# Projections of w_in as three products of scaled float16 parts instead of fp32r parts, with power-of-two scales found for four weight tiles at a time

## The chip, the cores and the metric

The kernel runs on one core of one Trainium2 chip. The metric is the device time of one execution, in microseconds (us). Engines are named as in the profile: PE is TensorE, with PEld for its weight loads, DVE is VectorE, ACT is ScalarE, POOL is GpSimd, and SP is SyncE, which here only issues transfers. Each engine runs its own instructions in the order in which they stand; ACT and POOL also issue transfers from their own queues.

## The reference

One encoder block over 1040 tokens (16 meta tokens and 1024 of x), width 1024. What the change touches is the first product, `proj`, of the normalized tokens with `w_in`, 1024 by 9280, and the five things cut from it:

```python
u = rms_norm(h, w_norm_mix[l])
proj = jnp.einsum('btd,dk->btk', u, w_in[l])
conf_a, conf_g = proj[..., 0:1024], proj[..., 1024:2048]
z, xbc = proj[..., 2048:4096], proj[..., 4096:7168]
dt_raw, gates = proj[..., 7168:7232], sigmoid(proj[..., 7232:])
c = silu(layer_norm(depthwise_conv(conf_a * sigmoid(conf_g), w_conf_dw[l], b), ...))   # 31 taps
branch_conf = einsum('btc,cd->btd', c, w_conf_out[l])
xbc = silu(depthwise_conv(xbc, w_ssm_conv[l], b))                                       # 7 taps
y = bidir_ssd(xs, dt_raw, ...)          # chunked scan over 9 chunks, both directions, 4 groups of 8 heads
branch_ssm = einsum('btc,cd->btd', rms_norm(y * silu(z), w_ssm_norm[l]), w_ssm_out[l])
h = h + einsum('btd,de->bte', gates[:1024] * branch_conf + gates[1024:] * branch_ssm, w_out[l])
h = h + expert_choice_ffn(rms_norm(h, ...), ...)        # 16 experts, 130 tokens each
return rms_norm(h[:, 16:], w_norm_final)
```

All inputs and the output are float32.

## The kernel before

The program is written in the order of the stages below, and a scheduler (it has its own model of the machine) fixes the order of the instructions on each engine before the run; `high_priority(offset=n)` lets it place work as if it had been written n steps earlier. On the chip each engine then runs its list in that order and waits by semaphores.

**Start.** Nine token tiles (`TOK`: 16, then 8 times 128) are loaded as `xt`, the odd ones from ACT's queue, the even ones from SP's. ACT squares each (`scr`, `ss`), DVE scales it, PE transposes it (`tp`), and it is split into two parts: `uh`, ACT's copy of the transpose in fp32r, and `ul`, DVE's difference (lines 186 and 187).

**Projection stage.** A weight tile is 1024 rows by 128 columns of `w_in`, held as 128 x 8 x 128. `load_w` (line 143, SP's queue, pool `wraw` of three) loads it, and `split_w` turns it into `wh` (ACT, line 151) and `wl` (DVE, line 152) in pool `wsp`, which has two of each. `proj` then makes, for each of three chunks of tokens (348, 346, 346), the 24 matmuls of `mm3`: for each of 8 slices, wh x uh, wh x ul, wl x uh (lines 96 to 98), all into one of the three PSUM buffers `mm`. 45 tiles come first: the dt tile, then four rounds of two conformer tiles (`do_conf`), six xbc tiles (`do_xbc`), two gate tiles and one z tile. The results leave PSUM by ACT (`pre`, `sg`, `st`) or DVE (`ci`). DVE does the convolutions: 30 taps over 1040 columns for each conformer tile (line 235, `co<-ci`), spread between other work by `some_taps`, and six for each xbc tile (line 340, `po<-pre`).

**Scan stage.** Four groups, each nine steps of two directions (`half`, at high priority). A half loads `row` (SP's queue, a broadcast of `cs_d`) and `xk`, `Bk` (ACT's queue); ACT makes `E` from `row` (lines 428 and 429), DVE multiplies `E` and `row` (lines 447 and 432), PE makes `cb`, `py` and `st_ps`, DVE and POOL carry the state `S`. After each step one item of `filler` is written: the other 28 weight tiles (4 conformer pairs, 12 z, 8 gates), in the program's order conformer, z, gates of that group. At the end of a group DVE multiplies by the z rows (`row<-row,xs`) and stores `yz_d`.

**After the scan.** `y_group` reloads `yz_d` rows as `yst` (two buffers, ACT's queue), splits each to `yh` (ACT) and `yl` (DVE), squares it (ACT) and adds it to `ssq` (POOL). `w_ssm_out` (32 tiles of 512 rows) and `w_conf_out` go through `load_w` and `split_w` as above and through `mm3` in fp32r. Beside it DVE does the conformer's layer norm (`mean`, `var`, `cc`). Then come `w_out`, the router, and 16 experts, whose products already use scaled float16 parts.

Names for the places spoken of later: the *last conformer tile* is the one of group 3, the *last gates* are two gate tiles written behind it, and the *hand-over* is the stretch from the last projection of `w_in` to the first product of `w_ssm_out`.

## Time and profile before

| | us |
|---|---|
| three timed runs | 3055.07, 3058.41, 3068.24; median 3058.41 |
| profiled execution, its own time | 3062.95 |
| its span, first to last instruction | 3061.2 |
| PE busy in the span | 2830.0 (92%) |
| DVE busy | 2216.2 (72%) |
| ACT busy | 1578.6 (52%) |

The span falls into stages: the start to about 42 us, projections to about 580, a pass of 25 us into the scan, the scan from about 605 to 1226, the hand-over and `w_ssm_out`, `w_conf_out`, `w_out` and the router to about 1700, then the experts to 3000. A busy share over the whole span mixes these, so the rows below are taken stage by stage. Matmuls are pipelined: a matmul's own duration covers more than its share of PE, and what counts is the distance between the starts of matmuls that follow each other.

### The profile page before, as it was taken

The page shows a single profiled execution, that of the slowest core. Times are in us where ns is not written, and L with a number is a line of the kernel's source. Part 1 is how long each engine was busy: PE and PEld are TensorE (multiplying, and loading weights), DVE is VectorE, ACT ScalarE, POOL GpSimd, SP SyncE. Part 2 cuts the span into 40 slices and gives each one's busy share as a digit, 9 for nine tenths or more (in the row PEclk, how much of TensorE's full clock was granted, in tenths as well). Part 3 has the DMA queues.
Part 4 walks back from the last instruction along what each step waited for, and adds up shares of the span by engine and source line. Part 5 has one row for each costly group of instructions (what it writes and reads, how often), then busy time and mean ns, then how long its engine had stood idle before and what let it go on. Part 6 is the DMA issues. An engine that isn't in the chain of part 4 may idle for free. (4 is left out here: it accounts for less than half of the span.)

```text
span 3061.2 us, 65630 instructions
## 1 busy us (share of the span) xinstructions
PE 2830.0 (92%) x28079; PEld 2693.4 (88%) x28079; DVE 2216.2 (72%) x2703; ACT 1578.6 (52%) x2351; POOL 722.2 (24%) x661
## 2 busy tenths in 40 slices
PE   7999999898888888899999789999999999999996
PEld 7999999786777676898978789999999999999995
DVE  7958669498696886989545678666767677767673
ACT  4433333454645564444213466666666666666643
POOL 1101011154354545322000002121222222222213
PEclk9999999899999899999999899999999999999998
DMA  4324233666868786442433879999999999999994
GB/s 123 108 90 133 72 124 99 165 144 167 183 170 205 178 192 133 156 141 80 154 119 115 298 285 327 320 320 328 329 325 339 330 324 333 332 321 333 343 325 139
DMA packets 425971, 665.99 MB, mean 218 GB/s; under 512 B 29217, under 2 KB 213953, under 8 KB 425673
## 3 DMA queue, kind: packets, MB, share of 16 engines
q1 hardware_dynamic: 366032, 514.83, 53.2%
q0 software_dynamic: 25760, 73.27, 7.9%
q10 hardware_dynamic: 33888, 73.71, 7.5%
q8 instruction: 220, 3.60, 0.5%
q14 instruction: 71, 0.58, 0.1%
HBM read 585.15 MB, written 76.59 MB: 216 GB/s over the span
## 5 line engine op out<-in xcount | busy, mean ns | idle before, releaser
L96 PE MATMUL gu<-xT,wh 128*128 128x130 f16 x3968 | 703.9, 223 | 4.3 <-ACT sil L952 3.8
L97 PE MATMUL gu<-xT,wh 128*128 128x130 f16 x3968 | 703.5, 221 | 0.0
L98 PE MATMUL gu<-xT,wl 128*128 128x130 f16 x3968 | 702.8, 221 | 0.6 <-DVE wl L923 0.4
L909 ACT ACTIVATE junk<-wst 128x2048 bf16<-128x2048 f32 x248 | 473.7, 1910 | 388.8 <-DMA wst<-in_w_exp_gate_dram 311.9
L96 PE MATMUL mm<-uh,wh 128*128 128x346 f32 (+2 forms) x1752 | 582.9, 333 | 14.5 <-ACT wh L151 12.2
L923 DVE SCALAR_TENSOR_TENSOR wl<-wst,sc,wh 128x2048 f16<-128x2048 f32 x248 | 572.8, 2346 | 24.2 <-ACT wh L920 21.0
L97 PE MATMUL mm<-ul,wh 128*128 128x346 f32 (+2 forms) x1752 | 579.7, 331 | 0.3 <-DVE ul L187 0.3
L98 PE MATMUL mm<-uh,wl 128*128 128x346 f32 (+2 forms) x1752 | 578.5, 331 | 0.2 <-DVE wl L152 0.2
L975 PE MATMUL dn<-ac,wst 128*128 128x130 f32 x3840 | 459.8, 277 | 0.0
L975 PEld LDWEIGHTS dn<-ac,wst 128*128 128x128 f32 x3840 | 441.1, 191 | 0.0
L97 PEld LDWEIGHTS <-wh 128*128 128x128 f16 x3968 | 394.4, 99 | 8.3 <-issue 6.8
L994 POOL DMA_INDIRECT h<-yo,idx x60 | 181.7, 3029 | 921.3 <-DVE yo L993 770.6
L96 PEld LDWEIGHTS <-wh 128*128 128x128 f16 x3968 | 388.9, 98 | 2.6 <-ACT wh L920 2.4
L98 PEld LDWEIGHTS <-wl 128*128 128x128 f16 x3968 | 386.6, 97 | 0.9 <-DVE wl L923 0.9
L96 PEld LDWEIGHTS mm<-uh,wh 128*128 128x128 f32 x1752 | 336.2, 192 | 29.4 <-ACT wh L151 14.0
L97 PEld LDWEIGHTS mm<-ul,wh 128*128 128x128 f32 x1752 | 336.6, 192 | 12.8 <-issue 11.8
L98 PEld LDWEIGHTS mm<-uh,wl 128*128 128x128 f32 x1752 | 335.5, 192 | 11.6 <-issue 10.4
L235 DVE SCALAR_TENSOR_TENSOR co<-ci,cp,co 128x1040 f32<-128x1040 f32 x240 | 343.1, 1429 | 1.7
L428 ACT ACTIVATE E<-row,cst 128x128 f32<-128x128 f32 (+1 forms) x576 | 170.2, 378 | 190.2 <-DMA row<-cs_d 171.7
L920 ACT ACTIVATE wh<-wst,sc 128x2048 f16<-128x2048 f32 x124 | 241.2, 1995 | 23.5 <-DVE sc L886 22.8
L151 ACT ACTIVATE wh<-wr 128x1024 fp32r<-128x1024 f32 (+1 forms) x113 | 105.6, 934 | 243.6 <-PE mm L97 196.1
L420 POOL TENSOR_TENSOR xw<-xk,dtw 128x512 f32<-128x512 f32 (+1 forms) x136 | 190.9, 1408 | 168.5 <-DMA xk<-xk_d 81.8
(329 smaller groups left out, 4572.1 us busy)
## 6 DMA issues: line engine op xcount, KB each, us to landing
wst<-in_w_exp_gate_dram SPq DMA_DIRECT2D x128, 1024.0 KB, 7.9
wst<-in_w_exp_up_dram SPq DMA_DIRECT2D x128, 1024.0 KB, 10.3
wst<-in_w_exp_down_dram SPq DMA_DIRECT2D x128, 1024.0 KB, 8.8
wr<-in_w_in_dram SPq DMA_DIRECT2D x73, 512.0 KB, 4.7
row<-cs_d SPq DMA_DIRECT2D x64, 512.0 KB, 9.0
xk<-xk_d ACTq DMA_DIRECT2D x64, 256.0 KB, 5.7
xbc_d<-po POOLq DMA_DIRECT2D x24, 520.0 KB, 3.0
xk_d<-xt POOLq DMA_DIRECT2D x20, 512.0 KB, 3.9
```

Source lines behind the costliest of these rows:

```text
L96: pe.matmul(ps, wh(k), xh(k), start=(k == 0), stop=False)
L97: pe.matmul(ps, wh(k), xl(k), start=False, stop=False)
L98: pe.matmul(ps, wl(k), xh(k), start=False, stop=(k == K - 1))
L151: act.activation(out=wh[:, :K], in_=r, func=AF.Copy)
L235: dve.scalar_tensor_tensor(co, ci[:, m:m + T], cp[:, j, m:m + 1], co, op0=OP.mult, op1=OP.add)
L420: pool.tensor_mul(heads(o[:L]), heads(xk[:L]), dtw[:L, c, w, hs].unsqueeze(2).to_broadcast([L, HG, 64]))
L428: act.activation(out=E[:L, j, :L], in_=row[:L, j, :L], func=AF.Relu, scale=-1.0, bias=cs)
L909: act.activation(out=junk, in_=t[m][b], func=AF.Square, accum_out=sq[:, b, m:m + 1])
L920: act.activation(out=wh[m][0], in_=t[m][0], func=AF.Copy, scale=sc[:, 1, m:m + 1])
L923: dve.scalar_tensor_tensor(wl[m][b], t[m][b], sc[:, 1, m:m + 1], wh[m][b], op0=OP.mult, op1=OP.subtract)
L975: pe.matmul(last["dn"][b // 3][:, b % 3], t[:, k, b * P:b * P + P], ac[:, 2 * i + k], start=(i + k == 0 and b % 3 == 0), stop=(i == 7 and ...
L994: nc.gpsimd.indirect_dma_start(out=h2_d[b], in_=yo[:, h], in_offset=None, compute_op=OP.add, out_offset=bass.IndirectOffsetOnAxis(ap=r.idx ...
```

## The change

The token parts and the weight parts of the 73 tiles of `w_in` become float16. To keep them in float16's range, each is multiplied by a power of two first: the tokens by one from the largest `w_norm_mix` (`power`, tile `su`), each weight tile by one from the sum of its squares. The class `Columns` holds the order of all 73 tiles. `group` loads four tiles (SP's queue, pool `r16` of eight), squares each on ACT with an accumulated sum, sums over partitions with one small PE matmul, and derives the scales with six small DVE instructions. `convert` makes `wh` and `wl`. `take` converts one tile ahead and asks for a group one group ahead. The inverse scale goes into instructions that already scale or copy (tanh, the copies of dt and xbc, the taps through `ct`, the z rows through `zinv`). `w_ssm_out` and `w_conf_out` keep fp32r and `split_w`; their pool `wsp` is now opened after the scan stage instead of at the start.

```diff
     wraw = wstack.enter_context(tpool("wraw", bufs=3))
-    wsp = wstack.enter_context(tpool("wsp", bufs=2))
...
+    def power(dst, src, up, down):
+        dve.tensor_scalar(dst[:, down], src, 32.0, 2.0 ** -110, op0=OP.mult, op1=OP.max)
...
-        uh = upool.tile([P, KD, T], FR, name="uh")
-        ul = upool.tile([P, KD, T], FR, name="ul")
+        uh = upool.tile([P, KD, T], F16, name="uh")
+        ul = upool.tile([P, KD, T], F16, name="ul")
...
+            def group(self):
+                b = 4 * self.groups
+                cols = self.order[b:b + 4]
...
+                for i, col in enumerate(cols):
+                    t = r16.tile([P, KD, P], F32, name="wr16")
+                    nc.sync.dma_start(t, w_in[0][:, col:col + P].rearrange("(k p) c -> p k c", p=P))
+                    act.activation(out=junk, in_=t, func=AF.Square, accum_out=sq[:, i:i + 1])
+                    self.raw[b + i] = t
+                sqb = w16.tile([P, 4], BF, name="sqb")
+                dve.tensor_copy(sqb[:, :n], sq[:, :n])
+                ps = mps.tile([P, 512], F32, name="mm")
+                pe.matmul(ps[:, :n], onesb, sqb[:, :n], start=True, stop=True)
...
+            def convert(self, n):
...
+                with tc.high_priority(offset=400):
+                    act.activation(out=wh, in_=t, func=AF.Copy, scale=sc[:, 1:2])
+                    dve.scalar_tensor_tensor(wl, t, sc[:, 1:2], wh, op0=OP.mult, op1=OP.subtract)
+                self.split[n] = wh, wl, sc
+
+            def take(self, col):
...
+                if n == 0:
+                    self.group()
+                    self.convert(0)
+                if n % 4 == 0:
+                    self.group()
+                self.convert(n + 1)
...
+        r16 = ostack.enter_context(tpool("r16", bufs=8))
+        w16 = ostack.enter_context(tpool("w16", bufs=2))
...
+            act.activation(out=wabs, in_=wmix, func=AF.Abs)
...
-                    act.activation(out=uu, in_=ps[:, :, :L], func=AF.Copy)
-                    dve.tensor_sub(ul[:, 4 * q:4 * q + 4, t0:t0 + L], ps[:, :, :L], uu.bitcast(F32))
+                    act.activation(out=uu, in_=ps[:, :, :L], func=AF.Copy, scale=su[:, 0:1])
+                    dve.scalar_tensor_tensor(ul[:, 4 * q:4 * q + 4, t0:t0 + L], ps[:, :, :L], su[:, 0:1], uu,
+                                             op0=OP.mult, op1=OP.subtract)
...
+    wsp = wstack.enter_context(tpool("wsp", bufs=2))
     right = ctx.enter_context(ExitStack())
```

**Start, ACT.** ACT's list while the first full token tiles are transposed and copied, before:

```order
L186 ACTIVATE uh<-tp 128x4x128
L151 ACTIVATE wh<-wr 128x1024
L186 ACTIVATE uh<-tp 128x4x128
L174 DMA xt<-in_x_dram 128x1024
L186 ACTIVATE uh<-tp 128x4x128 x2
L177 ACTIVATE scr,ss<-xt 128x1024
L186 ACTIVATE uh<-tp 128x4x128
```

And now, with numbers on the weight tiles (`wr_495` to `wr_504` are the first group, `wr_523` to `wr_532` the second):

```order
L192 ACTIVATE junk,sq<-wr_501 128x1024
L277 ACTIVATE uh<-tp,su 128x4x128 x2
L192 ACTIVATE junk,sq<-wr_504 128x1024
L277 ACTIVATE uh<-tp,su 128x4x128
L192 ACTIVATE junk,sq<-wr_523 128x1024
L277 ACTIVATE uh<-tp,su 128x4x128
L265 DMA xt<-in_x_dram 128x1024
L192 ACTIVATE junk,sq<-wr_526 128x1024
L217 ACTIVATE wh<-wr_495,sc 128x1024
L217 ACTIVATE wh<-wr_498,sc 128x1024
L217 ACTIVATE wh<-wr_501,sc 128x1024
L192 ACTIVATE junk,sq<-wr_529 128x1024
```

Squares of weight tiles now stand between the token copies; one more square of the second group, two of the third and four of token tiles follow before the next token copy.

**Start, PE.** Before, the first product of `w_in` stood behind the transposes of the first tokens:

```order
L184 MATMUL tp<-ident,xt 128x16 x8
L184 MATMUL tp<-ident,xt 128x128 x20
L96 MATMUL mm<-uh,wh 128x272
L184 MATMUL tp<-ident,xt 128x128 x4
L97 MATMUL mm<-ul,wh 128x272
```

Now both first groups' sums of squares stand ahead of it:

```order
L275 MATMUL tp<-ident,xt 128x16 x8
L275 MATMUL tp<-ident,xt 128x128 x24
L197 LDWEIGHTS onesb
L197 MATMUL mm<-sqb,onesb 128x4
L197 LDWEIGHTS onesb
L197 MATMUL mm<-sqb,onesb 128x4
L96 LDWEIGHTS wh
L96 MATMUL mm<-uh,wh 128x272
```

The first product moved behind the squares of eight weight tiles.

**Hand-over, DVE.** The list of DVE from the last conformer tile's `ci` on; `co<-ci` are its 30 taps, `wl<-wr,wh 128x512` is a tile of `w_ssm_out`. Before:

```order
L230 SCALAR_TENSOR_TENSOR ci<-sg,mm 128x346
L152 TENSOR_TENSOR wl<-wr,wh 128x1024
L235 SCALAR_TENSOR_TENSOR co<-ci,cp,co 128x1040 x4
L565 SCALAR_TENSOR_TENSOR yl<-yst,cp,yh 128x1040
L235 SCALAR_TENSOR_TENSOR co<-ci,cp,co 128x1040
L565 SCALAR_TENSOR_TENSOR yl<-yst,cp,yh 128x1040
L235 SCALAR_TENSOR_TENSOR co<-ci,cp,co 128x1040
L152 TENSOR_TENSOR wl<-wr,wh 128x512
L235 SCALAR_TENSOR_TENSOR co<-ci,cp,co 128x1040 x3
```

Now, from the first `yl` on (directly ahead of it stand the same `ci` and 17 taps):

```order
L663 SCALAR_TENSOR_TENSOR yl<-yst,cp,yh 128x1040
L329 SCALAR_TENSOR_TENSOR co<-ci,ct,co 128x1040
L663 SCALAR_TENSOR_TENSOR yl<-yst,cp,yh 128x1040
L329 SCALAR_TENSOR_TENSOR co<-ci,ct,co 128x1040 x5
L663 SCALAR_TENSOR_TENSOR yl<-yst,cp,yh 128x1040
L329 SCALAR_TENSOR_TENSOR co<-ci,ct,co 128x1040
L663 SCALAR_TENSOR_TENSOR yl<-yst,cp,yh 128x1040
L329 SCALAR_TENSOR_TENSOR co<-ci,ct,co 128x1040 x5
L663 SCALAR_TENSOR_TENSOR yl<-yst,cp,yh 128x1040
L329 SCALAR_TENSOR_TENSOR co<-ci,ct,co 128x1040
L663 SCALAR_TENSOR_TENSOR yl<-yst,cp,yh 128x1040 x2
L159 TENSOR_TENSOR wl<-wr,wh 128x512 x2
```

The first `wl` of `w_ssm_out` stood behind 6 taps and 2 `yl`; it now stands behind all 30 taps (17 and the 13 shown) and 7 `yl`. The pool `wsp` now lies where the scan stage's tiles lay: in the built program its first `wl` occupies bytes 46368 to 50464 of a partition, and `ci` bytes 47392 to 51672.

## Rows read from the trace of the kernel before

**Rows 1.** Windows by stage: length, busy us (instructions) by engine, PEclk, DMA, GB/s.
```profile
0.00:42.00 42.00, 26.60 (x182) 23.83 (x182) 30.51 (x52) 28.20 (x54) 10.62 (x110) 1.00 0.66 185
42.00:580.00 538.00, 536.06 (x3420) 531.72 (x3421) 407.87 (x354) 186.91 (x297) 54.83 (x133) 1.00 0.34 104
605.00:1226.00 621.00, 529.60 (x4124) 453.40 (x4125) 499.91 (x619) 339.92 (x786) 305.10 (x261) 0.93 0.74 173
1226.00:1250.00 24.00, 24.00 (x153) 24.00 (x153) 22.48 (x16) 10.43 (x13) 8.34 (x5) 1.00 0.64 204
1250.00:1300.00 50.00, 40.40 (x229) 39.25 (x228) 49.30 (x34) 23.19 (x37) 19.81 (x7) 0.90 0.41 128
```
**Rows 2.** Windows, wh x uh matmuls alone (line 96): PE, PEld, clock, DMA.
```profile
42.00:580.00 538.00, 346.75 (x1072) 201.61 (x1072) 1.00 0.34 104
605.00:1226.00 621.00, 204.13 (x582) 116.07 (x583) 0.93 0.74 173
```
**Rows 3.** Waits of PE from 42 to 580: waiter, releaser, total, times, longest.
```profile
PE mm L96 <- ACT wh L151: 1.9, 5, 0.4
```
**Rows 4.** Timeline of PE, projections, 348 and 346 columns: start, duration, what.
```profile
299.77 0.32 PE L97 MATMUL mm<-ul,wh 128*128 128x348 f32 x1
...
305.97 0.32 PE L97 MATMUL mm<-ul,wh 128*128 128x346 f32 x1
```
**Rows 5.** Timeline of PE, the dt tile's first chunk, 272 columns.
```profile
20.19 0.29 PE L98 MATMUL mm<-uh,wl 128*128 128x272 f32 x1
...
22.83 0.29 PE L98 MATMUL mm<-uh,wl 128*128 128x272 f32 x1
```
**Rows 6.** Timeline of PE, an expert's float16 products, 130 columns.
```profile
2630.16 0.22 PE L96 MATMUL gu<-xT,wh 128*128 128x130 f16 x1
...
2630.96 0.22 PE L98 MATMUL gu<-xT,wl 128*128 128x130 f16 x1
```
**Rows 7.** Costliest groups by form, ACT: count, busy, mean ns, idle before.
```profile
L151 ACT ACTIVATE wh<-wr 128x1024 fp32r<-128x1024 f32 x81 | 85.5, 1056 | 198.3 <-PE mm L97 168.5 <-DMA row<-sz_d 12.6 <-POOL xw L420 8.8
L177 ACT ACTIVATE scr<-xt 128x1024 f32<-128x1024 f32 x8 | 8.5, 1058 | 1.9 <-DMA xt<-in_x_dram 1.6 <-DVE xt L179 0.2
L177 ACT ACTIVATION_READ_ACCUMULATOR scr<-xt 128x1 f32 x8 | 1.6, 194 | 0.0
```
**Rows 8.** The same for DVE.
```profile
L923 DVE SCALAR_TENSOR_TENSOR wl<-wst,sc,wh 128x2048 f16<-128x2048 f32 x248 | 572.8, 2346 | 24.2 <-ACT wh L920 21.0
L152 DVE TENSOR_TENSOR wl<-wr,wh 128x1024 fp32r<-128x1024 f32 x81 | 108.6, 1341 | 67.5 <-ACT wh L151 67.1 <-PE mm L98 0.2
L888 DVE TENSOR_SCALAR sc<-sc,sx 128x2 f32<-128x2 f32 x62 | 13.9, 224 | 0.0
```
**Rows 9.** Timeline of PE, the first conformer product.
```profile
42.39 0.43 PE L96 MATMUL mm<-uh,wh 128*128 128x348 f32 x1 [0.18 <-ACT wh L151]
```
**Rows 10.** Waits of SP's queue from 605 to 1226, the largest.
```profile
SPq L143 <- DVE wl L152: 126.5, 19, 19.4
```
**Rows 11.** Waits of ACT from 605 to 1226, the largest.
```profile
ACT E L428 <- DMA row<-cs_d: 157.9, 49, 10.5
```
**Rows 12.** Waits of PE from 605 to 1226, the largest.
```profile
PE py L454 <- DVE E L447: 18.3, 13, 5.9
```
**Rows 13.** Timeline of DVE at the hand-over.
```profile
1227.35 0.52 DVE L230 SCALAR_TENSOR_TENSOR ci<-sg,mm 128x346 f32<-128x346 f32 x1 [0.15 <-PE mm L98]
...
1235.52 1.30 DVE L565 SCALAR_TENSOR_TENSOR yl<-yst,cp,yh 128x1040 fp32r<-128x1040 f32 x1 [0.84 <-ACT st L249]
```
**Rows 14.** Windows, the taps alone (line 235): DVE, clock, DMA.
```profile
1226.00:1250.00 24.00, 13.87 (x9) 1.00 0.64 204
1250.00:1300.00 50.00, 37.16 (x21) 0.90 0.41 128
```
**Rows 15.** Timeline of ACT, first `yh` of the first two pairs.
```profile
1233.48 1.17 ACT L564 ACTIVATE yh<-yst,cp 128x1040 fp32r<-128x1040 f32 x1 [1.60 <-DMA yst<-yz_d]
1246.01 1.17 ACT L564 ACTIVATE yh<-yst,cp 128x1040 fp32r<-128x1040 f32 x1 [3.02 <-DMA yst<-yz_d]
```

More of the change, by code (lines that the diff above doesn't have):

```diff
@@ new lines, in tile_block @@
+        order = [OFF_DT]
+        for i in range(4):
+            order += [i * P, D + i * P]
+            for m, j in enumerate((4 * i, 4 * i + 1, 4 * i + 2, 4 * i + 3, 16 + i, 20 + i)):
+                order.append(OFF_XBC + j * P)
+                if m in (2, 5):
+                    order.append(OFF_GATE + (2 * i + (m == 5)) * P)
+            order.append(OFF_Z + i * P)
+        for g in range(GR):
+            order += [(4 + g) * P, D + (4 + g) * P]
+            order += [OFF_Z + j * P for j in range(4 + 4 * g, min(8 + 4 * g, 16))]
+            order += [OFF_GATE + j * P for j in range(8 + 2 * g, 10 + 2 * g)]
@@ L168, in tile_block @@
+        columns = Columns(order)
+        wtile = columns.take
+        r16 = ostack.enter_context(tpool("r16", bufs=8))
+        w16 = ostack.enter_context(tpool("w16", bufs=2))
         with tpool("a_sb", bufs=2) as sb, tpool("a_ps", bufs=4, space=PSUM) as aps:
@@ L227, in do_conf @@
                 sg = cfp.tile([P, 348], F32, name="sg", bufs=2)
-                act.activation(out=sg[:, :n], in_=pg, func=AF.Tanh, scale=0.5)
+                act.activation(out=sg[:, :n], in_=pg, func=AF.Tanh, scale=wg[3])
                 pa = proj(wa, t0, n)
@@ L248, in gate_tile @@
                 ps = proj(w, t0, n)
-                act.activation(out=st[:, t0:t0 + n], in_=ps, func=AF.Tanh, scale=0.5)
+                act.activation(out=st[:, t0:t0 + n], in_=ps, func=AF.Tanh, scale=w[3])
             nc.gpsimd.dma_start(gate_d[j], st)
@@ L335, in do_xbc @@
                     ps = proj(w, t0, n)
-                    act.activation(out=pre[:, 3 + t0:3 + t0 + n], in_=ps, func=AF.Copy)
+                    act.activation(out=pre[:, 3 + t0:3 + t0 + n], in_=ps, func=AF.Copy, scale=w[2])
                 po = b1.tile([P, T], F32, name="po")
```

69 lines of the change are left out of this document (54 added, 15 removed).

## The prediction

> **What bounds the kernel now.** I read the windows by stage first, then the waits of the engine that is full, then the distances between its matmuls. The projection stage from 42 to 580 us is PE's alone: PE is busy 536.06 of 538 us at full clock [rows 1] and waits 1.9 us in all [rows 3]. DVE, at 407.87 us, is 76% busy beside it. In the scan, 605 to 1226, no engine is full: PE 529.60 of 621 us (85%), DVE 499.91 (80%), ACT 339.92 (55%) [rows 1]. There the halves follow each other through ACT, DVE and PE in turn, and the projections fill gaps. ACT's largest wait is for the `row` transfers, 157.9 us [rows 11], and SP's queue, which issues them, stands 126.5 us before weight loads whose buffer is not yet free [rows 10]. At the hand-over DVE is the full one: 49.30 of 50 us, with PE at 40.40 [rows 1].
>
> **The matmuls.** All 24 matmuls of a chunk keep their columns; what changes is the distance of their starts. In fp32r, 39 distances take 305.97 - 299.77 = 6.20 us, so 159.0 ns at about 347 columns [rows 4]. In float16 the trace has 130 columns only: 14 distances in 0.80 us, 57.1 ns [rows 6]. At one column per 1/2.4 ns, 130 columns are 54.2 ns, which leaves 2.9 ns. If that remainder is fixed, 346.7 columns take 144.4 + 2.9 = 147.4 ns; if everything grows with the columns, 57.1 x 346.7/130 = 152.4 ns. In fp32r the remainder is 125.7 - 113.3 = 12.4 ns at 272 columns (21 distances in 2.64 us [rows 5]) and 159.0 - 144.4 = 14.6 at 347: it grows, but by less than the columns do. I take 148.5, near the fixed end, so 10.5 ns per matmul, with 6.6 and 11.6 as bounds.
> The Trainium skill, "TensorE: Matmul & The Clock Gate", section "Wait — 56ns, not 53.3ns?", has the columns at 2.4 GHz and a fixed part of about 2.5 ns for a warm 16-bit matmul. The 130-column row agrees with it within half a nanosecond, and no row of this trace shows a wide one. By that rule the distance would be 146.9, and the projection stage alone would give 39 us instead of the 34 taken below.
>
> **Projection stage.** 3 x 1072 matmuls [rows 2] x 10.5 ns = 34 us less (bounds 21 and 37). All of it counts, since PE is full and nothing else ends there. What the change adds lies beside it. Per tile ACT squares 1024 columns: 1.06 + 0.19 us [rows 7], with 186.91 us of 538 busy before [rows 1]; 45 more of these make about 243 of 504, still under half. DVE's new `wl` is 2.35/2 = 1.17 us by the float16 row of twice the width, against 1.34 before [rows 8]. Each group of four adds seven small DVE instructions, at most 0.22 us each [rows 8], so 11 x 1.6 = 17 us. DVE then has about 418 us of work in 504, 83%. That is the cover of all these edits. If it fails, PE waits for `wl` or for a PSUM buffer that DVE has still to empty (the small sum takes one of the three `mm` buffers as well); I add nothing, and let it stand in the range. The tap, tanh and copy instructions that take another scale keep their width and count, at nothing.
>
> **Start.** Before the last token copy, ACT's list gains one `Abs` (1.06 us), 11 squares of weight tiles (11 x 1.25) and one more `wh` (1.06) [rows 7], 15.9 us together. ACT had 42 - 28.20 = 13.8 us idle in this stretch [rows 1], most of it before the first weights arrive, when the new work has no data either. PE's list puts the sums of eight weight tiles ahead of the first product, and PE works in order, so the dt tile, its copies on ACT and the transposes behind it all wait for the square of the eighth tile; before, they went between the tokens. On SP's queue eight weight loads and three of `w_ssm_out` now stand ahead of the fifth and seventh token tile. The first conformer product starts at 42.39 [rows 9]. Walking ACT's new list with these durations, I take 14 us later; bounds 2 (all idle filled) and 18.
>
> **Scan.** 3 x 582 matmuls [rows 2] x 10.5 ns = 18 us less on PE. With PE at 85%, I count half, 9 us. The second gain is in the queue. Eight buffers of raw weights mean that a load finds its buffer free, so SP does not hold `row` loads behind it; ACT gets `E` started sooner, and PE's 18.3 us of waits for `E` [rows 12] are what is near enough to profit. SP's other waits (for PE to release `row`, for `cbm`) stay, and become the late ones. I take 10 us. Against it: 28 squares of 1.25 us on ACT, in the same list as `E`; I take them as hidden in the 281 us in which ACT idles. Together 19 us less; bounds 53 less (18 + 35 of PE's 91 us of idle) and 25 more.
>
> **Hand-over.** The last two gates take PE's stretch 1226 to 1250, 153 matmuls, 1.6 us less [rows 1]. Then a wait is added. The first `wl` of `w_ssm_out` is written where `ci` lies, so it must follow the last conformer tile's 30 taps, and DVE's list has 7 `yl` there too. Behind it in DVE's list stand the layer norm's means; PE waits for it with all of `w_ssm_out`. Taps cost 51.03/30 = 1.70 us there [rows 14] and a `yl` 1.30 [rows 13]: 51 + 9 = 60 us from the last `ci` (bound: 30 x 1.3 + 9 = 48 if no tap is slowed). ACT's side gives the same: the `yst` loads now stand behind the last gate's tanh, pairs of `yh` come 1246.01 - 1233.48 = 12.5 us apart [rows 15], and the seventh is the first of the fourth pair, 3 x 12.5 + 4 to 6 us after the gates. The gates end 6 chunks x 24 x 148.5 ns = 21 us after `ci`. So PE stands idle for 60 - 21 + 1 = 40 to 44 us, I take 42, where it now starts `w_ssm_out` at once. But it loses 50 - 40.40 = 9.6 us in the next 50, and some clock [rows 1], because taps hold up `wl`; with the taps done, that comes back, 12 us. Net 30 us more; bounds 48 - 21 - 12 = 15 and 44.
>
> **Sum.** -34 (projections) + 14 (start) - 19 (scan) - 2 (gates) + 30 (hand-over) = -11 us. The profiled execution took 3062.95 us (1.75 outside its span of 3061.2) and would become 3052; it lies 4.5 us above the median of the three runs, 3058.41, so I predict 3047. A measurement of this kernel can tell about 0.5%, 15 us, from no change.
>
> **Rivals.**
> *The scan is let loose.* SP's 126.5 us before weight loads [rows 10] are as large as ACT's wait for `row` [rows 11], which speaks for it; against it, PE waits directly for `E` only 18.3 us, and DVE is at 80%. The scan would give 53 instead of 19: -45, 3013.
> *ScalarE orders the scan, and the kernel is slower.* The 28 squares are 28 x 1.25 = 35 us in the list that makes `E`, and one that is placed ahead of an `E` delays the whole half. For it: ACT is the first engine of each half. Against: it idles 45% there, and halves have high priority. If the scan gains nothing, the sum is +8; from 7 us of these 35 on the path the kernel is slower than can be told from none. With half of them there it is +25: 3083.
> *The products hardly get faster.* At 152.4 ns, 6.6 ns per matmul, the projections give 21 and the scan 16: -11 + 13 + 3 = +5, 3063. For it: fp32r's remainder does grow with the columns. Against: the row of 130 columns.
>
> **Chances.** The forecast, four terms near the values taken, 0.43 (3032 to 3062 by itself); the scan let loose 0.25; ScalarE 0.19; products hardly faster 0.13. Faster by over 0.5% (under 3043): 0.25 of the second and 0.17 of the first, 0.42. Slower by over 0.5% (over 3074): 0.16 of the third and 0.05 of the others, 0.21. The rest, 0.37. The range of 3010 to 3083 takes in the second case and the price of the third, and leaves out what lies past them.
>
> **What the next profile would show.** Projection matmuls at 147 to 149 ns; the first conformer product near 56 us; the stage from there to the scan about 34 us shorter, with PE still full. In the scan, SP's wait for weight buffers gone. At the hand-over, one gap of about 40 us on PE between the last `mm<-uh` and the first `wl` of `w_ssm_out`, with DVE full of taps. The forecast is wrong if PE shows waits in the projection stage (DVE or the `mm` buffers have become the bound), if the scan changes by more than its bounds, or if the gap is under 25 us.

## The result, and the profile after

The changed kernel takes 3106.94 us (median of 4 runs, 3092.43 to 3112.4) against 3058.94 for the kernel before beside it: ratio 1.0145, 95% interval 1.0104 to 1.0186. It is slower by some 1.5%, where 3047 was predicted (a second set of runs of it, e5_after below, gave 1.0%). The profiled execution took 3112.4 us, with a span of 3110.7, 49.5 more than before's.

Windows by stage of the changed kernel: start, projection stage, scan, last gates, hand-over, and the first 61 us of `w_ssm_out`. Columns as in [rows 1].

```profile
0.00:62.00 62.00, 29.67 (x178) 21.15 (x179) 36.97 (x71) 42.52 (x78) 10.68 (x110) 0.94 0.71 189
62.00:580.00 518.00, 511.86 (x3513) 345.72 (x3513) 414.39 (x438) 254.49 (x412) 65.33 (x145) 1.00 0.38 115
587.00:1240.00 653.00, 526.92 (x4135) 346.38 (x4136) 507.52 (x664) 359.54 (x811) 314.41 (x269) 0.87 0.69 160
1240.00:1261.00 21.00, 21.00 (x145) 13.95 (x143) 19.19 (x16) 4.00 (x6) 2.04 (x3) 1.00 0.32 116
1261.00:1309.00 48.00, 0.92 (x5) 0.53 (x3) 37.03 (x23) 15.99 (x16) 19.23 (x8) 0.54 0.36 104
1309.00:1370.00 61.00, 60.86 (x367) 59.68 (x367) 29.96 (x25) 25.38 (x46) 10.85 (x4) 0.97 0.43 146
```

PE is full in the projection stage, as before, and stands still for the whole hand-over (0.92 of 48 us). In the scan PE does about as much busy time as before in 32 us more, at a lower clock (0.87 for 0.93 in [rows 1]). Between the same marks in both traces (the first conformer product, the first `cb`, the last gated product `yz`, the last product with `uh`, the first and last with `yh`) the difference is:

| stretch | before | after | difference | predicted |
|---|---|---|---|---|
| start, to the first conformer product | 42.4 | 62.4 | +20.0 | +14 |
| projection stage, to the first `cb` | 562.0 | 524.1 | -37.9 | -34 |
| scan, to the last `yz` | 622.8 | 654.0 | +31.2 | -19 |
| last gates | 22.6 | 20.7 | -1.9 | -2 |
| idle before `w_ssm_out` | 0.1 | 47.4 | +47.3 | +42 |
| `w_ssm_out`, first to last start | 307.1 | 304.0 | -3.1 | -12 |
| all behind it | 1504.2 | 1498.0 | -6.2 | 0 |

The products: PE's timeline in the projection stage (start, duration, what), 17 distances in 2.49 us, 146.5 ns each, for 159.0 in [rows 4].

```profile
297.79 0.31 PE L96 MATMUL mm<-uh,wh 128*128 128x346 f16 x1
...
300.28 0.31 PE L98 MATMUL mm<-uh,wl 128*128 128x346 f16 x1
```

The waits of the scan, 587 to 1240 us (waiter, releaser, total, times, longest): ACT, SP's queue and PE.

```profile
ACT E L524 <- DMA row<-cs_d: 183.3, 45, 16.3
...
ACT junk L192 <- DMA wr<-in_w_in_dram: 20.4, 6, 13.7
```

```profile
SPq L512 <- DMA yz_d<-row: 94.3, 8, 32.7
SPq L191 <- DVE wl L218: 79.9, 15, 13.7
```

```profile
PE py L550 <- DVE E L543: 46.2, 13, 12.3
```

ACT waits for `row` 25 us more than in [rows 11], PE for `E` 28 us more than in [rows 12]. SP's wait for weight buffers is smaller than in [rows 10], 79.9 for 126.5, but not gone. New is `junk`, the output of the squares: ACT stands before a square whose weight tile has not landed, 20.4 us in six places, up to 13.7 in one, and every `E` behind it in the list stands too. The costliest groups by form show what the 73 squares take of ACT in the whole kernel (count, busy, mean ns, idle before); 17 of them fall into the scan, where the prediction had counted 28:

```profile
L192 ACT ACTIVATE junk<-wr 128x1024 bf16<-128x1024 f32 x73 | 76.9, 1054 | 123.5 <-DMA wr<-in_w_in_dram 119.1 <-POOL xw L516 4.3
...
L192 ACT ACTIVATION_READ_ACCUMULATOR junk<-wr 128x1 f32 x73 | 13.7, 187 | 0.0
```

The hand-over, PE's one wait between 1240 and 1310, and the timelines of DVE and ACT there:

```profile
PE mm L96 <- ACT wh L158: 47.1, 1, 47.1
```

```profile
1240.46 0.51 DVE L322 SCALAR_TENSOR_TENSOR ci<-sg,mm 128x346 f32<-128x346 f32 x1
1242.29 22.70 DVE L329 SCALAR_TENSOR_TENSOR co<-ci,ct,co 128x1040 f32<-128x1040 f32 x17 [1.32 <-ACT co L326]
...
1297.61 1.30 DVE L329 SCALAR_TENSOR_TENSOR co<-ci,ct,co 128x1040 f32<-128x1040 f32 x1
...
1309.26 1.29 DVE L159 TENSOR_TENSOR wl<-wr,wh 128x512 fp32r<-128x512 f32 x2
```

```profile
1306.84 1.16 ACT L662 ACTIVATE yh<-yst,cp 128x1040 fp32r<-128x1040 f32 x1 [5.62 <-DMA yst<-yz_d]
1307.91 0.61 ACT L158 ACTIVATE wh<-wr 128x512 fp32r<-128x512 f32 x1
```

The last tap ends at 1298.9; ACT makes `wh` at 1307.9, behind a seventh `yh` that waited for its `yst`; `wl` follows at 1309.3. The profile names `wh` where the prediction had said `wl`: the list of ACT was the later of the two sides.

### The profile page after: what moved, and what is told of

It is laid out like the page before. It is cut to its first block, busy times and chain, and to the rows that moved or that the text cites. A ratio compares the mean times of both kernels' runs of the same rounds, so it can differ in the third digit from the quotient of the medians.

```text
span 3110.7 us, 65955 instructions
## 1 busy us (share of the span) xinstructions
PE 2787.0 (90%) x28098; PEld 2372.4 (76%) x28098; DVE 2231.9 (72%) x2849; ACT 1684.7 (54%) x2502; POOL 735.0 (24%) x677
## 5 line engine op out<-in xcount | busy, mean ns | idle before, releaser
L97 PEld LDWEIGHTS <-wh 128*128 128x128 f16 x5720 | 568.8, 99 | 108.5 <-issue 21.2
L96 PEld LDWEIGHTS <-wh 128*128 128x128 f16 x5720 | 562.7, 98 | 113.8 <-issue 17.0
L98 PEld LDWEIGHTS <-wl 128*128 128x128 f16 x5720 | 560.7, 98 | 102.2 <-issue 13.9
L96 PE MATMUL mm<-uh,wh 128*128 128x346 f16 (+2 forms) x1752 | 557.5, 318 | 1.5 <-ACT pre L432 0.9
L97 PE MATMUL mm<-ul,wh 128*128 128x346 f16 (+2 forms) x1752 | 557.0, 318 | 0.0
L98 PE MATMUL mm<-uh,wl 128*128 128x346 f16 (+2 forms) x1752 | 556.9, 318 | 0.0
L329 DVE SCALAR_TENSOR_TENSOR co<-ci,ct,co 128x1040 f32<-128x1040 f32 x240 | 344.6, 1436 | 3.3 <-ACT co L326 1.3
L96 PE MATMUL mm<-yh,wh 128*128 128x346 f32 (+1 forms) x480 | 159.5, 332 | 63.4 <-ACT wh L158 48.5
L550 PE MATMUL py<-E,xw 128*64 128x128 f32 (+1 forms) x1152 | 126.7, 301 | 85.4 <-DVE E L543 46.2
L436 DVE SCALAR_TENSOR_TENSOR po<-pre,sp,po 128x1040 f32<-128x1040 f32 x144 | 184.8, 1294 | 2.6 <-ACT po L434 1.8
L543 DVE TENSOR_TENSOR E<-E,cbm 128x1024 f32<-128x1024 f32 (+1 forms) x72 | 97.6, 1355 | 94.9 <-ACT E L525 94.2
```

The source lines that it names most:

```text
L96: pe.matmul(ps, wh(k), xh(k), start=(k == 0), stop=False)
L97: pe.matmul(ps, wh(k), xl(k), start=False, stop=False)
L98: pe.matmul(ps, wl(k), xh(k), start=False, stop=(k == K - 1))
L329: dve.scalar_tensor_tensor(co, ci[:, m:m + T], ct[:, m:m + 1], co, op0=OP.mult, op1=OP.add)
L436: dve.scalar_tensor_tensor(po, pre[:, m:m + T], sp[:, j, m:m + 1], po, op0=OP.mult, op1=OP.add)
```

## The experiments

All runs, with the times of the stretches (us) from each one's profiled execution, and the ratio to the kernel before on the same chip. The mark between projection stage and scan is the first `cb`, before which PE stands 1.4 to 19.1 us in these runs for its load of `Ct`, and the last gates vary by some 20 us, so a difference in one stretch is to be read with the others. The column "to last `uh`" has no such marks in it: it runs from the first conformer product to the last product with `uh` (before: 1207.4, the changed kernel: 1198.8). ("None": products with `yh` began before the last with `uh`; e14_two_products leaves out products, and its last one comes before the scan's end.)

| run | start | projection stage | scan | to last `uh` | idle | median | ratio, 95% |
|---|---|---|---|---|---|---|---|
| e5_after | 61.6 | 522.6 | 654.8 | 1198.9 | 47.5 | 3094.1 | 1.0097 [1.0060, 1.0134] |
| e1_pools | 60.9 | 521.7 | 636.2 | 1178.8 | 0.0 | 3044.6 | 0.9981 [0.9964, 0.9999] |
| e2_const | 59.1 | 525.9 | 628.6 | 1176.5 | 44.1 | 3073.5 | 1.0082 [1.0059, 1.0106] |
| e3_arith | 50.4 | 527.2 | 616.2 | 1162.9 | 0.0 | 3011.5 | 0.9883 [0.9859, 0.9907] |
| e4_start | 61.4 | 524.3 | 633.1 | 1177.8 | 47.4 | 3083.9 | 1.0135 [1.0101, 1.0168] |
| e6_squares | 51.5 | 529.2 | 646.9 | 1192.8 | 0.1 | 3047.1 | 0.9955 [0.9934, 0.9976] |
| e8_const_pools | 57.1 | 527.8 | 626.8 | 1173.1 | 0.0 | 3036.4 | 0.9907 [0.9878, 0.9936] |
| e9_ready | 57.4 | 534.8 | 622.7 | 1176.4 | 0.0 | 3032.9 | 0.9935 [0.9912, 0.9958] |
| e13_pinned | 57.1 | 525.4 | 623.3 | 1174.7 | 0.0 | 3025.0 | 0.9908 [0.9882, 0.9935] |
| e12_arith_szbuf | 47.0 | 524.5 | 618.7 | 1182.0 | none | 3026.5 | 0.9927 [0.9900, 0.9954] |
| e14_two_products | 45.8 | 534.3 | 611.1 | - | - | 3016.5 | 0.9892 [0.9848, 0.9935] |
| e15_no_taps | 48.0 | 526.7 | 591.8 | 1177.1 | none | 3016.9 | 0.9893 [0.9846, 0.9939] |
| e7_moved | 58.5 | 554.0 | 617.4 | 1195.1 | 0.0 | 3054.8 | 0.9956 [0.9932, 0.9979] |
| e11_best | 52.7 | 541.9 | 613.4 | 1177.6 | 0.0 | 3029.0 | 0.9920 [0.9892, 0.9948] |
| e16_late | 61.2 | 531.8 | 589.4 | 1155.2 | 0.1 | 3015.9 | 0.9861 [0.9831, 0.9891] |
| e17_late_start | 59.5 | 535.1 | 622.5 | 1186.5 | 0.0 | 3040.1 | 0.9958 [0.9941, 0.9975] |

**The hand-over: e1_pools.**

```diff
-            tpool("bc") as bc, tpool("cfp") as cfp, ...
-        r16 = ...tpool("r16", bufs=8); w16 = ...
+        r16 = [tpool("r16a", bufs=4)]; cfp; w16; bc; r16.append(tpool("r16b", bufs=4))
```

> The changed kernel with its SBUF pools in another order, all else alike: the later float32r weight parts lie over the first group of raw weight tiles, not over the last conformer tile's ci and co. If the 47 us for which PE stands idle at the hand-over are the wait for the last tile's taps in that memory, the idle time between the last product with uh and the first with yh falls from 47.4 to under 6 us; the taps then run beside w_ssm_out as in the kernel before and slow it by 5 to 15 us, so the kernel gains 30 to 42 us on the changed one (about 3065 to 3077). If instead DVE's work there must be done first in any case, the idle time goes elsewhere and the time stays within 10 us. Start and scan stay as they are in the changed kernel under both (scan 654 us).

The idle time is gone. PE's largest wait from 1219 to 1300 is now

```profile
PE mm L98 <- DVE wl L159: 4.8, 3, 3.1
```

and `w_ssm_out`, with the taps beside it, takes 304.2 us, as much as behind them. So the 47 us went with the overlay. Whether the memory of the last tile held PE to the end, or the order of ACT's list that came with it (the last tap was done 9 us before `wh` was made), this run doesn't separate. By the two ratios, 1.0145 and 0.9981, the kernel gained some 50 us, more than the 30 to 42 expected: the scan, meant to be left alone, changed too, to 636.2.

**Is 654 the kernel's own scan: e5_after.**

> The changed kernel once more, unaltered, to see how far its scan differs from one execution to another. In the execution profiled first the scan (first cb to last yz) took 654.0 us, yet the runs with other pools and with the later loads at the start, whose scans are meant to be alike, took 636.2 and 633.1. If 654 is this kernel's own time, it comes back within 5 us; if it was that execution's, the scan comes out at 630 to 642 and the whole at 3080 to 3100, and of the 31 us that the scan lost only about 13 are the change's.

It is, to 0.8 us, in a second execution. So the scan's length belongs to the program as it was scheduled: other pools, which give other dependencies and another order, change it by 18 us with the same operations, and e4_start below, whose edit touches the start alone, by 21 (633.1). A difference of that size between two programs that also differ in order does not by itself show what made it; pairs that agree, and the ratios of the whole, have to bear it out.

**The start: e3_arith, e2_const, e4_start.** e2_const leaves `group()` only the four loads, and `sc` is one tile, filled once. e3_arith goes further:

```diff
-        t, sc = self.raw.pop(n)                 # groups of four, r16 of 8
+        t = load_w(w_in[0], self.order[n], KD)  # wraw of 3, as before
-        if n % 4 == 0: self.group()
-        self.convert(n + 1)
+        self.convert(n)
```

> The kernel before with only the arithmetic changed: float16 parts with a constant scale of 2^10, and the inverse scale applied where the changed kernel applies it; tiles loaded one at a time into the same three raw buffers, parts in two buffers, the float32r buffers of the later products where they were. It leaves out the squares, sums and loads of four. Theory 1 and theory 2 both expect the projection stage near 524 us, the scan at 595 to 615 (18 us of products less, of which half or more is seen), no idle PE at the hand-over, and the first conformer product within 4 us of 42.4: 3000 to 3015 in all. Theory 3 (the float16 parts, by DVE's dearer wl and the tanh with a scale from memory, slow the scan) expects the scan at 635 or more. If theory 1 holds, the scan of the run with the constant scale lies within 10 us of this one; if theory 2, that one lies 25 or more above this.

> The changed kernel with a constant weight scale of 2^10 (the value that these weights give): it leaves out the 73 squares on ScalarE, the 19 sums on PE and the scale arithmetic on DVE; loads of four tiles, buffers and products stay. Theory 1, the squares: in the scan they stand in ScalarE's list ahead of E and wait there for their loads, so the scan falls from 654 to 605 to 625 us, and the first conformer product comes 5 to 12 us sooner than 62.4. Theory 2, the transfers (four weight tiles at a time on SP's queue and the buffers' memory): the scan stays within 10 us of 654, and the start gains under 4. Theory 3, the float16 arithmetic itself: as theory 2 here. The hand-over keeps its 47 us of idle PE.

Together they split the 20 us: the arithmetic 8.0 (50.4 - 42.4; under 4 was expected), the loads of four 8.7 (59.1 - 50.4), the squares with their sums 3.3 (62.4 - 59.1). The split is good to some 5 us: three runs below with the start of e3_arith come out at 47.0, 48.0 and 45.8. That the 8.7 are traffic is argued, not shown: in the changed kernel SP's queue (start, duration, what) needs 19.5 us to hand out seven weight loads, and the fifth and seventh token tile stand behind them.

```profile
2.33 19.48 SPq L191 DMA_DIRECT2D wr<-in_w_in_dram  x7
21.86 3.52 SPq L142 DMA_DIRECT2D wr<-in_w_ssm_out_dram  x3
25.50 1.25 SPq L265 DMA_DIRECT2D xt<-in_x_dram  x2
```

Part of the 8.0 is the clock. PE starts later and with gaps, and in e3_arith the granted clock (a mean over its two levels, 2.4 and 1.2 GHz) then falls to 0.66 while PE is nearly full; [rows 1] have 1.00. In e12_arith_szbuf and e15_no_taps it is 0.83 from 30 to 40 us and 1.00 after, in e14_two_products 1.00 throughout, and their starts are shorter by 3.4, 2.4 and 4.6 us.

```profile
30.00:40.00 10.00, 9.08 (x43) 5.66 (x42) 7.64 (x11) 5.20 (x12) 1.24 (x3) 0.66 0.24 63
40.00:50.00 10.00, 9.63 (x71) 6.16 (x69) 4.42 (x11) 5.33 (x9) 0.20 (x4) 0.83 0.00 0
```

In the scan the two runs take 616.2 and 628.6: the arithmetic is not what slows it, and most of the loss is gone without squares, sums and scale arithmetic. The 12.4 between the two fall between the theories (under 10, or 25 and more). e4_start puts the second group's loads and squares and three loads of `w_ssm_out` behind the last token tile:

```diff
+        with tc.issue_after(xload.ins), tc.issue_after(tok.ins):   # group 1
             nc.sync.dma_start(t, ...); act.activation(out=junk, in_=t, func=AF.Square, ...)
```

> The changed kernel with the second group of four weight tiles (its loads on SP and its squares on ScalarE) and the first three loads of w_ssm_out placed behind the last token tile, all else alike. If the start's 20 us are the weight traffic and the squares ahead of the token tiles, the first conformer product comes at 46 to 54 instead of 62.4, and the kernel gains as much, 8 to 16 us (3090 to 3100). If it is the length of the first group's own chain (four loads, four squares, sum, scales, parts), the first conformer product stays within 4 us of 62. Scan and hand-over stay.

A miss: 61.4, so the question about the traffic stays open. The scheduler put all dt products behind the transposes, so the first product came at 47.5 instead of 36.4, and PE's clock was lower still:

```profile
20.00:40.00 20.00, 8.99 (x41) 7.19 (x41) 19.22 (x34) 18.26 (x34) 1.24 (x3) 0.57 0.70 206
```

**Squares or loads of four: e6_squares, e8_const_pools.** The first adds to e3_arith one line, the second is e2_const with e1_pools' order.

```diff
             t = load_w(w_in[0], self.order[n], KD)
+            act.activation(out=junk, in_=t, func=AF.Square, accum_out=sq)
```

> The run with the arithmetic alone (float16 parts, constant scale, single loads: 3011.5 us, scan 616.2), with one thing added: a square on ScalarE of every weight tile before its wh, 73 in all, whose result nothing uses. Theory 1 (squares on ScalarE's list delay E) expects the scan at 628 to 645 and the whole 15 to 30 us longer. Theory 2 (the loads of four make the scan's loss) expects the scan within 8 us of 616 and the whole within 10 us of 3011 to 3021 (the start's squares cost up to 4 of them).

> The constant weight scale and the other order of pools together, with loads of four: it leaves out squares, sums and scale arithmetic. Against the run with the other pools (3044.6 us, scan 636.2) it lacks only the squares and sums; against the run with the arithmetic alone (3011.5, scan 616.2) it has the loads of four, one tile ahead, in eight buffers. Theory 1 expects the scan within 8 us of 616 and the whole at 3012 to 3024; theory 2 expects the scan within 8 us of 636 and the whole at 3030 to 3045. A scan near 626 means both, in halves. No idle at the hand-over under either.

e6_squares: the scan rises from 616.2 to 646.9 by squares alone, and the ratio from 0.9883 to 0.9955. e8_const_pools: 626.8, in the middle; the loads of four may add 10, and squares, sums and scale arithmetic then 9.4 (ratio 0.9907 to 0.9981). ACT stands before squares in e6_squares too:

```profile
ACT junk L188 <- DMA wr<-in_w_in_dram: 15.3, 6, 6.0
```

**ScalarE's time, or its wait: e9_ready, e13_pinned, e16_late.** Both of the first two add squares of a resident tile (`uh`) to e8_const_pools, e13_pinned behind each `wh`:

```diff
-        act.activation(out=wh, in_=t, func=AF.Copy, scale=sc[:, 1:2])
+        h = act.activation(out=wh, in_=t, func=AF.Copy, scale=sc[:, 1:2])
+        with tc.issue_after(h.ins):
+            act.activation(out=junk, in_=uh[:, 0, 0:1024]..., func=AF.Square, accum_out=sq)
```

> The run with the constant scale and the other pools (3036.4 us; scan 626.8, of it 498.8 inside the four groups, from each group's first masked E to its last), with 73 squares on ScalarE put back, each where the changed kernel has it, but of a tile that has lain in SBUF since the start, so that a square never waits for a load; results unused. The squares of the weights cost 21 to 24 us inside the groups in three pairs of runs. If that is ScalarE's time (28 x 1.25 us in the list ahead of E), the groups come to 515 to 523 again. If it is ScalarE's list standing before a square whose weights have not landed (20 us of such waits in the changed kernel's scan), the groups stay at 499 to 507.

> The run with the constant scale and the other pools (3036.4 us, scan 626.8) with a square on ScalarE right behind each tile's wh, of a tile that has lain in SBUF since the start; result unused, 73 in all, 27 or 28 in the scan. They cannot move out of the scan and never wait for a load. If ScalarE's time is what the squares cost, the scan takes 640 to 655. If it is the waits for weights that have not landed, the scan stays at 618 to 632.

e9_ready told something else than asked: with data that is always there, all squares moved to the time before 180 us; the projection stage grew by 7.0 us and the scan not at all. In e13_pinned they were in the scan, 24 of them in ACT's window from 583 to 1206,

```profile
L213 ACT ACTIVATE junk<-uh 128x1024 bf16<-128x1024 f16 x24 | 25.0, 1041 | 0.0
L213 ACT ACTIVATION_READ_ACCUMULATOR junk<-uh 128x1 f32 x24 | 4.5, 187 | 0.0
```

and the scan stayed at 623.3, the ratio at 0.9908 for 0.9907. So in the whole, 29.5 us of ScalarE's time cost nothing here. The measure that the expectation of e9_ready names says otherwise: inside the four groups (from DVE's first `E<-E,cbm` of a group to its last) e13_pinned takes 520 us where e8_const_pools takes 498, as much as ScalarE's time was to cost, while the three changes of group fall from 115 to 91. But the same exchange happens without a square (e3_arith to e14_two_products: 502 to 528, and 100 to 74), so this split does not decide. e16_late asks from the other side: e1_pools with computed scales of the weights themselves, only later.

```diff
             if n % 4 == 0: self.load(g)                # four loads, no squares yet
             self.convert(n + 1)
+            if n % 4 in (1, 2): self.square(g, n % 4 * 2 - 2, n % 4 * 2)   # behind this wh
+            if n % 4 == 2: self.sums(g)
```

> The changed kernel with the pools in the other order (3044.6 us, scan 636.2), computed scales and loads of four as there; only the squares of a group stand later in ScalarE's list: two behind the wh of the third tile ahead of their group and two behind that of the second, when the loads, asked for two or three tiles earlier, have landed. If the squares cost the scan only by ScalarE standing before weights that have not landed, the scan falls to 615 to 629, ScalarE's waits for wr there from 21.7 us to under 6, and the kernel to 3025 to 3037. If their place in the list or their 35 us cost, the scan stays at 630 to 655.

The scan falls by 46.8 us, to 589.4, further than expected; with a projection stage 10.1 longer and last gates 13.0 longer, 23.7 are left to the last `uh`, and the ratio goes from 0.9981 to 0.9861. No wait of ACT for `wr` is left among the scan's, and those for `row` and for the `yz` stores fell with them. First ACT's and SP's waits in e1_pools, from 583 to 1219, then those of e16_late, from 593 to 1182:

```profile
ACT E L527 <- DMA row<-cs_d: 167.3, 45, 16.2
...
ACT junk L197 <- DMA wr<-in_w_in_dram: 21.7, 6, 13.9
```

```profile
SPq L515 <- DMA yz_d<-row: 84.3, 8, 28.2
```

```profile
ACT E L542 <- DMA row<-cs_d: 120.0, 44, 9.1
```

```profile
SPq L530 <- DMA yz_d<-row: 24.0, 6, 9.0
```

So late squares can end the loss. That the wait for the landing made it is not shown: e17_late_start below has late squares and no such wait either, and gains nothing clear of noise on e1_pools (0.9958 for 0.9981, with intervals that overlap; 1186.5 us to the last `uh` for 1178.8). Nor is it shown why the scan of e16_late is some 30 us shorter than in the runs without squares. What holds over all runs: the scan is over 630 us in every program that squares freshly loaded tiles in it ahead of their landing (633.1 to 654.8), and under 630 in every other. Part of that sits in the marks: to the last `uh` the two kinds overlap (1177.8 to 1198.9, and, for the others with float16 parts and all products, 1155.2 to 1195.1).

**What bounds the scan: e12_arith_szbuf, e14_two_products, e15_no_taps.** All change e3_arith.

```diff
-  sz = s2.tile([P, T], F32, name="row", bufs=4)      +  name="szr", bufs=2      # e12
-  mm3(...)   +  wh x uh, wh x ul alone if columns.at > 45                       # e14
-  taps.extend(...)   +  if j < 4: taps.extend(...)                              # e15
```

> The run with the arithmetic alone (3011.5 us, scan 616.2, of it 99.7 in the three changes from a group to the next, from its last masked E to the next group's first), with buffers of its own for the gated product sz, which shares the four row buffers there. If the next group's first E waits for its row, and that for a buffer which the yz stores still read, the three changes fall by 10 to 20 us each, to 45 to 70 together, and the kernel to 2970 to 2990. If they are set by what else is done there (the last taps and fillers, the loads of xs, Bt and Ct), they stay within 10 us of 100 and the time within 10 us of 3011.

> The run with the arithmetic alone (3011.5 us, scan 616.2) without the third product (low weight part by uh) in the 28 tiles of the scan and the hand-over: 672 matmuls of 147 ns less, 99 us of PE, some 86 of them in the scan; the rest of the computation stays. If PE's products bound the scan, it falls by 60 to 90 us. If the chain of the halves through ScalarE, VectorE and PE bounds it, it falls by under 20, and that would be why 18 us of faster products were not seen.

> The run with the arithmetic alone (3011.5 us, scan 616.2) without the 120 taps of the last four conformer tiles, which run on VectorE in the scan and at the hand-over: some 160 to 190 us of VectorE less, of its 510 in the scan. If VectorE bounds the scan, it falls by 60 us or more; if the chain or PE, by under 25 (an E or a row that comes later through a tap ahead of it costs about half a tap in each of 72 halves).

e12_arith_szbuf: the changes of group fall from 99.7 to 38.1 us, as the buffer theory had it, and the groups themselves grow by 53.1: the scan is 618.7. The time of the group change only moved, and the kernel is far from the 2970 to 2990 expected. e14_two_products: 672 matmuls less, and the scan falls by 5 us, with a projection stage 7.1 longer. The last product with `uh` is at 1063.7 there, and behind it PE is at 57% with the scan still running. The run's first row also answers another rival, that the lower granted clock made the changed kernel's scan long: at 0.85, below its 0.87, the scan is 43 us shorter.

```profile
580.00:1191.00 611.00, 456.16 (x3612) 302.69 (x3612) 543.42 (x654) 342.47 (x778) 307.82 (x262) 0.85 0.75 177
1064.00:1191.00 127.00, 72.33 (x588) 50.58 (x586) 111.54 (x135) 74.44 (x181) 65.05 (x52) 0.73 0.69 147
```

e15_no_taps: 140 us less of DVE (370.08 for 510.46) gives 24 us of scan, and nothing of the whole. By the expectation that is, just, the chain or PE. But the groups with their changes fall by 55 us, from 601 to 546; then 45 us instead of 14 pass from the last `E<-E,cbm` to the last `yz`, in which PE is full of projections (second row) and DVE's gated products wait for `sz_d` rows of z tiles.

```profile
575.00:1167.00 592.00, 492.01 (x3955) 320.17 (x3956) 370.08 (x529) 340.67 (x775) 279.02 (x260) 0.91 0.76 181
1122.00:1167.00 45.00, 44.63 (x332) 29.90 (x331) 15.97 (x22) 9.63 (x14) 3.36 (x7) 1.00 0.44 143
```

So PE's products alone do not bound the scan, and the taps hold up the halves by more than the 24 us tell; without them the leftover projections bound the end. That the chain of the halves is what remains is argued by leaving out; more `row` buffers for the halves themselves (SP waits 128.3 us there for PE to release one, in the changed kernel) were not tried.

**Versions with computed scales: e7_moved, e11_best, e17_late_start.** The first two load the scan's 28 tiles a second time in the projection stage for their squares, e7_moved on SP's queue, e11_best on GpSimd's, and load singly in the scan; e17_late_start is e16_late with the dt tile as a first group of its own and some loads behind the token tiles.

```diff
+  def ahead(self, k):      # e7: four of the 28 tiles, again, for their squares alone
+      self.load(ghost.tile(...), 45 + 4 * k + i); act.activation(out=junk, ..., func=AF.Square, ...)
+      self.scales(sq, 4, scg[k])
-      nc.sync.dma_start(t, ...)      +  nc.gpsimd.dma_start(t, ...)             # e11
+  self.load(0); self.square(0, 0, 1); ...; self.load(1)                         # e17
```

> A version with computed scales that means to beat both kernels: the pools in the order of the first experiment; the squares and sums of the 28 tiles of the scan done in the projection stage, on tiles loaded once more for it, so that in the scan each tile is loaded singly, one ahead, with its scale known; the first group is the dt tile alone, and the third group's and w_ssm_out's first loads stand behind the token tiles. Theory 1 expects the scan at 605 to 622, as theory 2 does (both the squares and the loads of four are gone from it); the projection stage at 524 to 530, since ScalarE and the transfers have room there; no idle at the hand-over; the first conformer product at 50 to 58: 3005 to 3025 in all. If the projection stage gets over 535 us, the second loading isn't hidden.

> A second version with computed scales: as the first (pools in the other order, the scan's 28 tiles squared and summed in the projection stage from a loading of their own, single loads in the scan, the first group the dt tile alone), but the second loading goes through GpSimd's queue, three tiles deep, each square is issued two tiles behind its load, and the third group's squares stand behind the last token tile on ScalarE. The first version lost 30 us in the projection stage (554 us), where ScalarE waited 100 us for weight loads behind one another on SP's queue. If that was the shared queue, the stage comes to 524 to 535, the scan stays at 612 to 628, and the whole at 3010 to 3030. If the stage stays over 545, it is the squares' place in ScalarE's list and not the queue.

> The late squares of the run beside this one, with the start of the last version (the first group is the dt tile alone; the third group's and w_ssm_out's first loads stand behind the token tiles on SP's queue; that start had its first conformer product at 52.7). Expected: first conformer product 50 to 56 instead of 60.9, projection stage 522 to 530, scan 615 to 629, no idle at the hand-over: 3012 to 3030, the best of the versions with computed scales, and below the kernel before by 20 to 40 us.

Both scans without squares come out as said, 617.4 and 613.4, but the projection stage pays, 554.0 and 541.9. GpSimd's queue gave back less than half, which lies between the two readings of e11_best's expectation. ACT's waits before squares are hardly it: in e7_moved they are 100.4 us from 59 to 612 (19.4 of them for the second loads, `wrg`), in the changed kernel 93.4 from 62 to 585, and there PE waits for ACT 1.9 us in all. With 28 more squares in ACT's list `po` and `pre` come late, which is 18.7 of the 30 us; PE's and ACT's waits in e7_moved, and the wait of ACT in the changed kernel:

```profile
PE xtp L476 <- ACT po L464: 13.1, 6, 5.0
PE mm L96 <- ACT pre L459: 5.6, 4, 3.7
```

```profile
ACT junk L216 <- DMA wr<-in_w_in_dram: 81.0, 29, 7.5
...
ACT junk L228 <- DMA wrg<-in_w_in_dram: 19.4, 10, 2.8
```

```profile
ACT junk L192 <- DMA wr<-in_w_in_dram: 93.4, 42, 5.4
```

e17_late_start has no wait before squares and a scan of 622.5, as expected, but no better start (59.5 for 50 to 56), its projection stage is 535.1, and at 3040.1 us it misses the 3012 to 3030 expected. Against e16_late, with squares in the same places behind the `wh`, it is 33 us longer in the scan, as e5_after and e1_pools differ by 18: what the order does beyond the waits named here stays open. The best version of all is e16_late, 1.4% faster than the kernel before; its interval overlaps that of e3_arith.

## Why the prediction was wrong

**Projection stage: right, a little past its bound.** -34 predicted (21 to 37 less), -37.9 measured; 3 x 1072 products x 12.5 ns would be 40. The distance of 146.5 ns lies below the 148.5 taken, and just below the 147.4 of the fixed end. The rule that was weighed there (the Trainium skill, "TensorE: Matmul & The Clock Gate", section "Wait — 56ns, not 53.3ns?") gave 146.9, and this trace now agrees with it (146.5). The cover held: DVE is 80% busy (414.39 of 518 us) and PE full. Two prices in it were too low: `wl` takes 1.45 us for 1.17, and a tanh with its scale from memory 0.53 us for 0.45 before, where nothing was added; behind a full PE neither shows.

**Scan: the step that failed.** It stood at -19 and was +31.2. Its three terms can be read from runs that add them one after the other, each with another order too, which alone is worth up to some 20 us. The faster products were to give 9: e3_arith has 6.6 less than before. The freer queue was to give 10: e2_const, with eight buffers and loads of four, has 12.4 more than e3_arith. The squares were to cost nothing: the changed kernel has 25.4 more than e2_const. Together that is the +31.2.

The first term was near its number, though by e14_two_products hardly for its reason: with 99 us of products taken away, the scan gives 5. In the second, a load was to find its buffer free: SP still waits 79.9 us for weight buffers (110.6 with three buffers in e3_arith), and its waits for the `yz` stores grew from 47.6 to 94.3; in before, from 604 to 1227 us:

```profile
SPq L416 <- DMA yz_d<-row: 47.6, 7, 25.6
```

The third is the largest miss, a cost put at nothing: the squares were "hidden in the 281 us in which ACT idles". Three pairs of runs give 30.7 (e6_squares less e3_arith, squares alone), 25.4 (the changed kernel less e2_const) and 9.4 us (e1_pools less e8_const_pools; these two with sums and scale arithmetic). An idle share does not say that added work falls into the idle time, in an engine that works in order. Whether the squares cost by their time in ACT's list or by standing before loads that have not landed (20.4 us in the changed kernel) stays open: e13_pinned speaks for the wait in the whole and for the time inside the groups, e16_late for the wait, e17_late_start against it. The rival "ScalarE orders the scan" named the right engine and sign, and its +25 was the price nearest to what came.

**Hand-over: right in mechanism, 14 us too low in its sum.** The idle time was 47.4 for 42, and went with the overlay (e1_pools). Of the 12 us that were to come back, 3.1 did. They had been read from PE's 40.40 of 50 us beside the taps [rows 1], and there they came: the first 61 us have PE at 60.86. But the term looked no further than the taps. Behind them DVE does the layer norm in two runs of 13.8 and 13.6 us, PE waits 14.9 us for DVE to take its results out of PSUM into `acc`, and the stretch still takes 304. PE's waits in `w_ssm_out` in before, 1250 to 1557 us, then in the changed kernel, 1309 to 1613, and DVE's two runs there:

```profile
PE mm L98 <- DVE wl L152: 11.7, 5, 5.7
PE mm L96 <- DVE acc L590: 4.0, 1, 4.0
```

```profile
PE mm L96 <- DVE acc L688: 14.9, 4, 6.5
PE mm L98 <- DVE wl L159: 1.2, 1, 1.2
```

```profile
1362.81 13.78 DVE L632 TENSOR_TENSOR cc<-cc,mean 128x1040 f32<-128x1040 f32 x8
...
1423.90 13.57 DVE L640 TENSOR_TENSOR cc<-cc,var 128x1040 f32<-128x1040 f32 x4
```

**Start: right in sign, 6 us too low.** ACT's list was priced (15.9 us of new work), and the squares are only some 3 of the 20. The loads of four, known from SP's list but not priced, cost about 9, and the arithmetic with its gaps and lower clock 3 to 8.

**The size.** +14 - 34 - 19 - 2 + 30 = -11 became +20.0 - 37.9 + 31.2 - 1.9 + 44.2 - 6.2 = +49.4. Of the 60 us between them 50 are the scan. The terms' own upper bounds (+18, +25, +44, with -34 and -2) make +51. That this is near what came is luck: start, scan and hand-over each passed their bound a little (20.0, 31.2, 44.2), and projections and the rest made up for it. But the range stopped at +25, as if only one of them could be reached at a time.

## What to carry to other kernels

An instruction added to an in-order engine has two prices, its duration and what it waits for, and both fall on what stands behind it in the list; an idle share over a stage covers neither by itself. Before counting a faster operation as a gain, ask whether the stage is bound by that engine: 12.5 ns per matmul was worth nearly all of itself where PE was full (37.9 of 40 us), and 6.6 of 22 us in a chain at 85%. When a pool is freed and another opened later, look at which late-living tile its memory held. And where a scheduler sets the order, an edit elsewhere can move a stage by 20 us: repeat a question in a second order before you believe the answer.

## What the runs showed of the hardware

- Float16 products of 346 columns stand 146.5 ns apart, 2.3 over the columns at 2.4 GHz; fp32r ones had 14.6 over them [rows 4].
- The granted clock of the start depends on more than the list of operations: from 30 to 40 us it is 0.66 in e3_arith, 0.83 in e12_arith_szbuf and 1.00 in e14_two_products (means over the two levels), with the same start operations and PE about 9 of 10 us busy. In e3_arith that is 10 x 0.34 + 10 x 0.17, an estimated 5 us; its start is 4.6 longer than e14_two_products'.
- SP's queue took 19.48 us to issue seven loads of 512 KB, with a DMA share of 1.11 from 2 to 22 us; the two token loads behind them went out at 25.5 us, in before at 8.6 and 17.7.
- A scan of 650 us repeated to 0.8 us in a second execution, yet the same operations with the pools in another order took 18 us less.
